# Fourteen products of zeros instead of seven, and another order of the selected branch's gathers, in a hybrid attention and state-space step

## The chip, the cores and the metric

The kernel runs on one core of one Trainium2 chip. The metric is the device time of one execution in microseconds (us), as the median of several runs. The core's engines are TensorE (PE: matrix products and transposes), VectorE (DVE), ScalarE (ACT), GpSimd (POOL) and SyncE (SP, which here only issues transfers). Each engine works through its own list of instructions in order and waits on semaphores for the others.

## The reference

One inference step of one layer for a prompt of 512 tokens and for 8 samples of 8 new tokens each, which share the weights. Cut to what matters:

```python
q, kc, vc, ksl, vsl, kwn, vwn, gn, za, u, zs, gm = split_in(h @ w_in)      # 1024 -> all parts at once
# attention of a sample: three branches, each with its own softmax
o_c = softmax(q @ compressed keys) @ compressed values      # compress(): chunks of the paged cache through a small MLP
o_s = softmax(q @ keys of the N_SEL best blocks) @ values   # "selected": rows of the second paged cache
o_w = softmax(q @ last 512 rows) @ values                   # "window"
a   = (g0 * o_c + g1 * o_s + g2 * o_w) * silu(z_att)
s   = GLU(GELU(S5(u))) * silu(z_ssm)                        # S5: complex diagonal state-space scan
x   = LayerNorm(ALPHA * x + W_o(sig(g_att) * (a @ P_att) + sig(g_ssm) * (s @ P_ssm)))
```

Everything is float32. The outputs are both groups' rows, the new key and value rows, the window's state and the S5 state.

## The kernel before, in words

All 576 rows (512 of the prompt, 64 of the samples) are held transposed. `load_x` loads five tiles `xp` of 128 rows, turns each with 8 transposes through the PSUM tile `p_tr` and splits the result into a high part `xTh` (ACT, line 108) and a low part `xTl` (DVE, line 121), because a product of float32 values is made of three products of such parts (`mm3`, `natural`). A weight tile goes the same way: `w_raw` loads `wraw` by a DMA of SP's queue (line 318; there are two such buffers), ACT makes `whi` of it, DVE `wlo`. `natural` (line 353) then makes 24 products for each row tile: four of `whi` with `xTh`, four of `whi` with `xTl`, four of `wlo` with `xTh`, and these twelve again for the second half of the inner dimension. The samples' rows take one unsplit product each (line 345, with `xTs`), straight from `wraw`.

At the very start, ahead of the first transposes, PE makes seven products of a tile `zero` of zeros (line 291) into a PSUM tile that nothing reads.

After that come, overlapping: the weights of `u` in two pieces and of the keys and values in three (`inproj_u`, `inproj_kv`; I call the last three A, B and C; the low part of B is made by POOL, and small copies `kvn`, line 390, are made by DVE in A), the S5 parameters and scan (loads at lines 490 to 509, a long chain of small operations on DVE), the rest of the in-projection, the prompt's attention (scores at lines 966 and 967), the compression of the cached pages (gathers `gc`, products at lines 129 to 131 with `evh`, `evl`), and for each pair `w` = 0 to 3 of samples `attend(w)`.

`attend(w)` handles two samples, b = 0 and 1. Its selected branch has two tiles per sample and step t, h = 0 and h = 1: `attend_gather` gathers them with four indirect DMAs of POOL's queue (line 1070) into tiles `g8`, of which five exist in all. `branch` goes through four groups; groups 0 and 1 use both samples' h = 0 tiles, groups 2 and 3 both samples' h = 1 tiles, first for the transposes of the keys (line 135) and scores (line 1192), then for the values (line 1201). A gather of step t = 1 waits until a tile of t = 0 has been read for the last time.

No order is written out by hand: the program is handed to a scheduler that sets the order of every engine's instructions from its own estimates of their durations. An edit at the start therefore moves instructions in the whole program.

Of the kernel before, what the change touches and what calls it, by code (L numbers as in the profile page):

```python
# [9 lines left out]
F = mybir.dt.float32  # L10
# [75 lines left out]
def rr(ap, pat, **kw):  # L86
    return ap.rearrange(pat, **kw)


class Hybrid:  # L90
# [41 lines left out]

    def tr(self, out, in_):
        k = in_.shape[0]
        self.nc.tensor.transpose(out, in_, self.ident[:k, :k])  # L135

    def psum(self, tag, shape, name=None):
        return self.ps.tile(shape, F, name=name or ("p_" + tag), tag=tag, bufs=self.psbufs[tag])
# [142 lines left out]
    def load_x(self):  # L281
        nc, A, pa = self.nc, self.A, self.pa
        self.xTh = pa.tile([128, 8, TOK], FR, name="xTh")
        self.xTl = pa.tile([128, 8, TOK], FR, name="xTl")
        self.xTs = pa.tile([128, 8, 64], F, name="xTs")

        z = self.p0.tile([128, 128], F, name="zero")
        nc.vector.memset(z[:], 0.0)
        p = self.psum("ca", [128, 128])
        for i in range(7):  # L290
            nc.tensor.matmul(p[:], z[:], z[:], start=True, stop=True)
        for i in range(5):
            m = 128 if i < 4 else 64
            src = rr(A["x_prompt"], "o (i p) c -> (o i) p c", p=128)[i] if i < 4 else rr(A["x_sample"], "b t c -> (b t) c")
            x = self.p0.tile([128, DM], F, name="xp", tag="xp", bufs=5)
            if i:
                nc.sync.dma_start(x[:m], src)
            else:
                for c in (slice(0, 512), slice(512, 1024)):
                    nc.sync.dma_start(x[:, c], src[:, c])  # L300
                self.wu = self.w_raw([(OFF_U, 256)], 2)
            for h in range(2):
                p = self.psum("tr", [128, 4, 128])
                for k in range(4):
                    self.tr(p[:, k, :m], x[:m, (4 * h + k) * 128:(4 * h + k + 1) * 128])
                v = slice(4 * h, 4 * h + 4), slice(i * 128, i * 128 + m)
                self.split(self.xTh[(slice(None),) + v], self.xTl[(slice(None),) + v], p[:, :, :m])
                if i == 4:
                    nc.vector.tensor_copy(self.xTs[:, 4 * h:4 * h + 4], p[:, :, :m])

# [955 lines left out]
    def attend_gather(self, w):  # L1266

        nc, A, pb = self.nc, self.A, self.pb
        wn = pb.tile([128, 2, 4, 256], F, name="wn", tag="g8", bufs=5)
        nc.gpsimd.dma_start(rr(wn[:], "q b k c -> q b (k c)"),  # L1270
                            rr(A["state_win_kv"], "b (q k) v g d -> q b (k v g d)", k=4)[:, 2 * w:2 * w + 2])
        yield wn
        for t in range(2):
            gs = []
            for b in range(2):
                for h in range(2):
                    gs.append(pb.tile([128, 8, 2, 2, 64], F, name="g8", tag="g8", bufs=5))
                    self.gather(gs[-1][:], "cache_kv_slc", self.idx2[:, h, t, 2 * w + b:2 * w + b + 1])
            yield gs[:2], gs[2:]

    def attend(self, w, store, gat):
        nc, A, pb = self.nc, self.A, self.pb
# [337 lines left out]
```

## Time and profile before

| what | value |
|---|---|
| median of 3 runs | 929.78 us (928.15 to 930.36) |
| the profiled execution | 930.57 us |
| its span, first to last instruction | 928.8 us |
| PE busy | 866.0 us, 93 % of the span |
| DVE, ACT, POOL busy | 626.4, 428.3, 224.7 us |
| mean granted TensorE clock | 0.967 of full speed |

The profiled execution's time is 1.8 us more than its span, for what lies around the instructions. PE is idle for 62.8 us of the span.

### The profile page before, as it was taken

To read this page: it belongs to the slowest core of one execution; us is meant where nothing else is said; L and a number is where in the kernel's file an instruction comes from. 1 tells how busy PE (TensorE), PEld (TensorE's weight loads), DVE (VectorE), ACT (ScalarE), POOL (GpSimd) and SP (SyncE) were. 2 spreads that over 40 slices of the span, in tenths; PEclk is the share of its full clock that TensorE was granted. 3 is DMA by queue.
4 is the path that set the end of the run, shared out by engine and by line. 5 is a ranking of instruction groups with operands and counts; after the bars stand their busy time and mean duration, and the time that the engine had idled before them with its cause. 6 is when DMAs were issued, how large, how long until landed. Compare 5 with 4: busy or idle time off the path is not lost.

```text
span 928.8 us, 18351 instructions
## 1 busy us (share of the span) xinstructions
PE 866.0 (93%) x7262; PEld 759.6 (82%) x7262; DVE 626.4 (67%) x1494; ACT 428.3 (46%) x872; POOL 224.7 (24%) x255
## 2 busy tenths in 40 slices
PE   8979999999999997999989898999999989998896
PEld 8979999899999976767777777777878778878785
DVE  3479855654444679998778777878884455347874
ACT  4214652432543546465545453555455666445410
POOL 0328285000301034211132302232321011106500
PEclk9999999999999996999999998999999989999999
DMA  8672543465962361413298627454743276756331
GB/s 267 140 202 78 163 97 103 161 207 150 297 211 72 107 207 58 147 61 98 80 323 242 232 101 273 136 177 187 272 136 123 74 260 207 257 136 197 113 102 46
DMA packets 109989, 151.02 MB, mean 163 GB/s; under 512 B 29464, under 2 KB 85128, under 8 KB 105552
## 3 DMA queue, kind: packets, MB, share of 16 engines
q1 hardware_dynamic: 84304, 69.74, 25.5%
q0 software_dynamic: 16544, 75.44, 23.2%
q10 hardware_dynamic: 9056, 4.67, 1.8%
q8 instruction: 57, 0.93, 0.4%
q14 instruction: 28, 0.23, 0.1%
HBM read 134.02 MB, written 19.93 MB: 166 GB/s over the span
## 4 chain that ended last, share of the span: by engine, by line
PE 53%; DVE 22%; DMA 11%; issue 4%; POOL 4%; ACT 4%; SPq 2%; DVEq 0%; ACTq 0%; POOLq 0%
DVE xt L872 10%; PE p_mm L130 8%; PE p_mm L129 8%; PE p_mm L131 8%; PE p_tr L135 6%; DMA g<-in_cache_kv_slc,idx 4%; PE p_S L1192 3%; DVE evl L121 3%; PE p_ca L129 2%; PE p_ca L130 2%; PE p_ca L131 2%; DMA wraw<-in_w_in 2%; DMA bt<-vD 2%; PE p_acc L1201 2%; PE p_mm L353 1%
## 5 line engine op out<-in xcount | busy, mean ns | idle before, releaser
L130 PE MATMUL p_mm<-evl,w1h 128*128 128x256 f32 (+1 forms) x512 | 156.2, 305 | 10.4 <-DVE evl L121 8.3
L129 PE MATMUL p_mm<-evh,w1h 128*128 128x256 f32 (+1 forms) x512 | 153.0, 299 | 2.1 <-ACT evh L108 2.1
L131 PE MATMUL p_mm<-evh,w1l 128*128 128x256 f32 (+1 forms) x512 | 150.7, 294 | 0.0
L872 DVE STREAM_TRANSPOSE xt<-gc 128x256 f32<-128x256 f32 x256 | 145.4, 636 | 1.5 <-DMA gc<-in_cache_kv_cmp,idx 1.0
L121 DVE TENSOR_TENSOR evl<-xt,evh 128x512 fp32r<-128x512 f32 x128 | 87.2, 687 | 55.6 <-ACT evh L108 55.2
L1070 POOL DMA_INDIRECT gc<-in_cache_kv_cmp,idx x64 | 64.2, 1004 | 246.8 <-DVE xt L872 188.4
L130 PEld LDWEIGHTS p_mm<-evl,w1h 128*128 128x128 f32 x512 | 101.5, 198 | 20.2 <-DVE evl L121 15.3
L108 ACT ACTIVATE evh<-xt 128x512 fp32r<-128x512 f32 x128 | 79.8, 628 | 80.2 <-PE p_mm L131 76.3
L129 PEld LDWEIGHTS p_mm<-evh,w1h 128*128 128x128 f32 x512 | 101.8, 199 | 8.5 <-ACT evh L108 5.4
L131 PEld LDWEIGHTS p_mm<-evh,w1l 128*128 128x128 f32 x512 | 101.7, 199 | 0.2
L129 PE MATMUL p_mm<-xTh,whi 128*128 128x288 f32 x272 | 80.8, 297 | 1.7 <-DVE zst L475 1.7
L130 PE MATMUL p_mm<-xTl,whi 128*128 128x288 f32 x272 | 81.1, 298 | 0.0
L131 PE MATMUL p_mm<-xTh,wlo 128*128 128x288 f32 x272 | 81.1, 298 | 0.0
L108 ACT ACTIVATE kt<-p_tr 128x512 f32<-128x512 f32 x72 | 41.4, 596 | 52.9 <-PE p_tr L135 52.7
L108 ACT ACTIVATE pt<-p_tr 128x512 f32<-128x512 f32 x76 | 43.0, 591 | 34.5 <-PE p_tr L135 34.5
L1070 POOL DMA_INDIRECT g<-in_cache_kv_slc,idx x32 | 30.9, 964 | 108.0 <-PE p_acc L1201 98.1
L121 DVE TENSOR_TENSOR wlo<-wraw,whi 128x2048 fp32r<-128x2048 f32 (+2 forms) x23 | 43.5, 1901 | 14.7 <-ACT whi L108 14.5
L129 PEld LDWEIGHTS p_mm<-xTh,whi 128*128 128x128 f32 x272 | 51.3, 189 | 2.0 <-DVE zst L475 2.0
L991 DVE CUSTOM_DVE_ANT_0 P<-p_S,bt 128x128 f32<-128x128 f32 (+3 forms) x64 | 30.1, 486 | 33.4 <-PE p_S L967 23.5
L130 PEld LDWEIGHTS p_mm<-xTl,whi 128*128 128x128 f32 x272 | 51.3, 189 | 0.2 <-issue 0.2
L131 PEld LDWEIGHTS p_mm<-xTh,wlo 128*128 128x128 f32 x272 | 51.4, 189 | 0.0
L108 ACT ACTIVATE whi<-wraw 128x2048 fp32r<-128x2048 f32 (+2 forms) x24 | 37.1, 1561 | 29.0 <-DMA wraw<-in_w_in 9.5
(526 smaller groups left out, 2168.0 us busy)
## 6 DMA issues: line engine op xcount, KB each, us to landing
wraw<-in_w_in SPq DMA_DIRECT2D x11, 1024.0 KB
wraw<-in_w_in SPq DMA_DIRECT2D x10, 512.0 KB
gD<-zst SPq DMA_DIRECT2D x16, 288.0 KB
tg<-gD SPq DMA_DIRECT2D x16, 288.0 KB
wn<-in_state_win_kv POOLq DMA_DIRECT2D x4, 1024.0 KB, 9.4
wor<-in_w_o SPq DMA_DIRECT2D x8, 512.0 KB
out<-in_state_win_kv SPq DMA_DIRECT2D x8, 504.0 KB
wraw<-in_w_in SPq DMA_DIRECT2D x3, 1056.0 KB
```

The costliest lines, as they stand in the source:

```text
L108: return self.nc.scalar.activation(out, in_, func, **kw)
L121: eng.tensor_tensor(lo, src, hi.bitcast(F), op=OP.subtract)
L129: mm(out, lhi, rhi, start=start, stop=False, **kw)
L130: mm(out, lhi, rlo, start=False, stop=False, **kw)
L131: mm(out, llo, rhi, start=False, stop=stop, **kw)
L135: self.nc.tensor.transpose(out, in_, self.ident[:k, :k])
L353: self.nc.tensor.matmul(p[:m, :n], a[:, k], w[:, k, :n], start=j == 0, stop=j == 23)
L872: self.nc.vector.transpose(out=out, in_=bass.AP(tensor=in_.tensor, offset=in_.offset, ap=[in_.ap[0], [1, 8], [st, 4], [8, 8]]))
L991: V.tensor_tensor_reduce(out=P4[:, r, :n], in0=p[:, :n], in1=back, scale=1.0, scalar=NEG, op0=OP.add, op1=OP.max, accum_out=mx[:, r:r + 1])
L1070: self.nc.gpsimd.indirect_dma_start(out=rr(out, "c s v g d -> c (s v g d)"), out_offset=None, in_=src, in_offset=bass.IndirectOffsetOnAxis ...
L1192: mm = self.nc.tensor.matmul(out[r], self.qb[:, w, r], keys[b], start=True, stop=True)
L1201: self.nc.tensor.matmul(acc[r], PT[:, r], vals(b)[:, g * 64:(g + 1) * 64], start=start, stop=stop, skip_group_check=True)
```

## The change

`tr` now returns its instruction. The seven products of zeros become ten, and four more are made behind the last transpose of the first row tile, held there by a dependency. `attend_gather` issues the gathers of a step in the order (b0,h0), (b1,h0), (b0,h1), (b1,h1); before it was (b0,h0), (b0,h1), (b1,h0), (b1,h1).

```diff
     def tr(self, out, in_):
         k = in_.shape[0]
-        self.nc.tensor.transpose(out, in_, self.ident[:k, :k])
+        return self.nc.tensor.transpose(out, in_, self.ident[:k, :k])
...
-        p = self.psum("ca", [128, 128])
-        for i in range(7):
-            nc.tensor.matmul(p[:], z[:], z[:], start=True, stop=True)
+        pz = self.psum("ca", [128, 128])
+
+        def warm(n, *behind):
+            for _ in range(n):
+                mm = nc.tensor.matmul(pz[:], z[:], z[:], start=True, stop=True)
+                self.after(mm, *behind)
+        warm(10)
...
-                    self.tr(p[:, k, :m], x[:m, (4 * h + k) * 128:(4 * h + k + 1) * 128])
+                    tr = self.tr(p[:, k, :m], x[:m, (4 * h + k) * 128:(4 * h + k + 1) * 128])
...
+                if i == 0 and h:
+                    warm(4, tr)
...
-            gs = []
-            for b in range(2):
-                for h in range(2):
-                    gs.append(pb.tile([128, 8, 2, 2, 64], F, name="g8", tag="g8", bufs=5))
-                    self.gather(gs[-1][:], "cache_kv_slc", self.idx2[:, h, t, 2 * w + b:2 * w + b + 1])
-            yield gs[:2], gs[2:]
+
+            gs = [[], []]
+            for h in range(2):
+                for b in range(2):
+                    gs[b].append(pb.tile([128, 8, 2, 2, 64], F, name="g8", tag="g8", bufs=5))
+                    self.gather(gs[b][-1][:], "cache_kv_slc", self.idx2[:, h, t, 2 * w + b:2 * w + b + 1])
+            yield gs
```

Lines behind `load_x` are six higher in the changed kernel (353 is 359, 318 is 324, 1070 is 1076).

The start of PE's list, before:

```order
L291 MATMUL p_ca<-zero 128x128 x7
L135 MATMUL p_tr<-cst,xp 128x128 x8
L353 MATMUL p_mm<-whi,xTh 128x256 x4
L353 MATMUL p_mm<-whi,xTl 128x256 x4
L353 MATMUL p_mm<-wlo,xTh 128x256 x4
L353 MATMUL p_mm<-whi,xTh 128x256 x4
L135 MATMUL p_tr<-cst,xp 128x128 x8
L353 MATMUL p_mm<-whi,xTl 128x256 x4
L353 MATMUL p_mm<-wlo,xTh 128x256 x4
L353 MATMUL p_mm<-whi,xTh 128x256 x4
L135 MATMUL p_tr<-cst,xp 128x128 x4
```

The same place in the changed kernel:

```order
L293 MATMUL p_ca<-zero 128x128 x10
L135 MATMUL p_tr<-cst,xp 128x128 x8
L293 MATMUL p_ca<-zero 128x128 x4
L359 MATMUL p_mm<-whi,xTh 128x256 x4
L135 MATMUL p_tr<-cst,xp 128x128 x4
L359 MATMUL p_mm<-whi,xTl 128x256 x4
L359 MATMUL p_mm<-wlo,xTh 128x256 x4
L359 MATMUL p_mm<-whi,xTh 128x256 x4
L135 MATMUL p_tr<-cst,xp 128x128 x4
L359 MATMUL p_mm<-whi,xTl 128x256 x4
L359 MATMUL p_mm<-whi,xTh 128x256 x4
L359 MATMUL p_mm<-wlo,xTh 128x256 x4
```

The second row tile's transposes have split in two and moved ahead of most of the first products, and four products of `whi` stand before the second `wlo`. On DVE the second `wlo` of this weight tile now stands behind two `xTl` instead of one.

SP's list where the third and fourth weight tiles are loaded (A and B of the keys and values), before; `a`, `dt`, `cn`, `b`, `dd` and `sn` are S5 parameters:

```order
L318 DMA wraw<-in_w_in 128x8x264
L490 DMA a_523<-in_ssm_a_re 32x64 x2
L490 DMA a_523<-in_ssm_a_im 32x64 x2
L493 DMA dt<-in_ssm_log_dt 128x32
...
L509 DMA sn<-in_state_ssm_im 128x128
L318 DMA wraw<-in_w_in 128x8x264
L664 DMA uc<-uD 32x1024 x8
L318 DMA wraw<-in_w_in 128x8x264
L664 DMA uc<-uD 8x1024 x4
```

The same place in the changed kernel:

```order
L324 DMA wraw<-in_w_in 128x8x264 x2
L496 DMA a_530<-in_ssm_a_re 32x64 x2
L496 DMA a_530<-in_ssm_a_im 32x64 x2
L499 DMA dt<-in_ssm_log_dt 128x32
...
L515 DMA sn<-in_state_ssm_im 128x128
L670 DMA uc<-uD 32x1024 x4
L324 DMA wraw<-in_w_in 128x8x264
L670 DMA uc<-uD 32x1024 x4
```

Tile B's load has moved ahead of all S5 loads, and C's load is now in front of the last four of the eight loads of `uc` (the rows of `u`, read back from memory).

POOL's list where step t = 1 of the first pair is gathered, before (`g8_5419` is b0,h0; `g8_5421` is b0,h1; `g8_5423` is b1,h0; `g8_5425` is b1,h1; `gc` are gathers of the compression):

```order
L1070 DMA g8_5419<-in_cache_kv_slc,idx2_496 128x2048
L1070 DMA gc_6769<-in_cache_kv_cmp,idx4_503 128x1024 x2
L1070 DMA gc_6772<-in_cache_kv_cmp,idx4_503 128x1024 x2
L1070 DMA g8_5421<-in_cache_kv_slc,idx2_496 128x2048
L1070 DMA g8_5423<-in_cache_kv_slc,idx2_496 128x2048
L1070 DMA g8_5425<-in_cache_kv_slc,idx2_496 128x2048
L1270 DMA wn_6289<-in_state_win_kv 128x2x1024
L1070 DMA gc_6775<-in_cache_kv_cmp,idx4_503 128x1024 x2
L1070 DMA gc_6778<-in_cache_kv_cmp,idx4_503 128x1024 x2
```

The same place in the changed kernel (`g8_5426` is b0,h0; `g8_5428` is b1,h0; `g8_5430` is b0,h1; `g8_5432` is b1,h1):

```order
L1076 DMA g8_5426<-in_cache_kv_slc,idx2_503 128x2048
L1076 DMA gc_6776<-in_cache_kv_cmp,idx4_510 128x1024 x2
L1076 DMA gc_6779<-in_cache_kv_cmp,idx4_510 128x1024 x2
L1076 DMA g8_5428<-in_cache_kv_slc,idx2_503 128x2048
L1076 DMA g8_5430<-in_cache_kv_slc,idx2_503 128x2048
L1076 DMA gc_6782<-in_cache_kv_cmp,idx4_510 128x1024 x2
L1076 DMA gc_6785<-in_cache_kv_cmp,idx4_510 128x1024 x2
L1076 DMA g8_5432<-in_cache_kv_slc,idx2_503 128x2048
L1276 DMA wn_6296<-in_state_win_kv 128x2x1024
```

The tile (b1,h0) has moved from third to second of its four, and (b1,h1) from directly behind the third to behind four more gathers of the compression. Elsewhere the order changes throughout: on PE, the first row of prompt scores (line 966 before, 972 after) moves from row 1044 to row 1242 of its list and the last from row 2046 to row 2147, while the first product of the compression moves from row 1682 to row 1650. The transposes of the S5 parameters `a` and `cn` (line 135) move from rows 63, 64 and 66 to rows 83, 91 and 95, of which most rows hold four products.

## Rows read from the trace of the kernel before

**Rows 1.** The page, busy time of TensorE.

```profile
PE 866.0 (93%) x7262; PEld 759.6 (82%) x7262; DVE 626.4 (67%) x1494; ACT 428.3 (46%) x872; POOL 224.7 (24%) x255
```

**Rows 2.** Waits of PE, whole span: total us, times, longest.

```profile
...
PE p_S L966 <- DVE amx L991: 7.8, 8, 2.8
PE p_tr L135 <- DMA g<-in_cache_kv_slc,idx: 4.9, 4, 2.3
PE p_mm L353 <- DVE kvn L390: 3.7, 1, 3.7
```

**Rows 3.** Order of time on PE, 0 to 16 us: start, duration, what.

```profile
1.06 3.36 PE L291 MATMUL p_ca<-zero 128*128 128x128 f32 x14 [1.06 <-DVE zero L288]
5.19 1.94 PE L135 MATMUL p_tr<-cst,xp 128*128 128x128 f32 x8 [0.77 <-DMA xp<-in_x_prompt]
8.84 1.22 PE L353 MATMUL p_mm<-whi,xTh 128*128 128x256 f32 x4 [1.71 <-ACT whi L108]
...
11.56 1.05 PE L353 MATMUL p_mm<-whi,xTh 128*128 128x256 f32 x4
12.42 1.77 PE L135 MATMUL p_tr<-cst,xp 128*128 128x128 f32 x8
...
14.97 0.64 PE L353 MATMUL p_mm<-whi,xTh 128*128 128x256 f32 x4
15.45 0.60 PE L135 MATMUL p_tr<-cst,xp 128*128 128x128 f32 x4
```

**Rows 4.** Order of time on ACT, 5 to 11 us.

```profile
7.73 1.06 ACT L108 ACTIVATE whi<-wraw 128x1024 fp32r<-128x1024 f32 x1 [0.82 <-DMA wraw<-in_w_in]
```

**Rows 5.** Order of time on DVE, 5 to 13 us.

```profile
9.96 0.68 DVE L121 TENSOR_TENSOR xTl<-p_tr,xTh 128x512 fp32r<-128x512 f32 x1
10.56 1.22 DVE L121 TENSOR_TENSOR wlo<-wraw,whi 128x1024 fp32r<-128x1024 f32 x1
```

**Rows 6.** Order of time on SP's queue, 30 to 66 us.

```profile
33.50 0.37 SPq L318 DMA_DIRECT2D wraw<-in_w_in  x1
...
36.50 0.42 SPq L493 DMA_DIRECT2D dt<-in_ssm_log_dt  x1
...
51.40 0.38 SPq L318 DMA_DIRECT2D wraw<-in_w_in  x1
51.97 11.69 SPq L664 DMA_DIRECT2D uc<-uD  x8
```

**Rows 7.** Order of time on PE, 38 to 73 us.

```profile
42.08 1.97 PE L345 MATMUL p_mm<-wraw,xTs 128*64 128x128 f32 x32
...
60.27 0.77 PE L353 MATMUL p_acc<-whi,xTh 128*128 128x264 f32 x4 [1.40 <-ACT whi L108]
...
65.23 1.25 PE L353 MATMUL p_mm<-whi,xTh 128*128 128x264 f32 x4 [3.73 <-DVE kvn L390]
```

**Rows 8.** Order of time on DVE and ACT, 33 to 69 us.

```profile
41.42 0.18 DVE L529 TENSOR_SCALAR w<-dt 128x32 f32<-128x32 f32 x1 [7.53 <-DMA dt<-in_ssm_log_dt]
...
58.25 1.96 ACT L108 ACTIVATE whi<-wraw 128x2112 fp32r<-128x2112 f32 x1 [6.71 <-DMA wraw<-in_w_in]
...
61.17 3.83 DVE L573 TENSOR_TENSOR w<-w,w 128x32 f32<-128x32 f32 x1
```

**Rows 9.** Busy us by stretch, PE, PEld, DVE, ACT, POOL; then granted clock.

```profile
65.10:72.00 6.90, 6.64 (x28) 6.33 (x29) 6.90 (x41) 0.09 (x1) 0.95 (x1) 0.51 0.60 190
...
350.00:400.00 50.00, 42.46 (x249) 35.96 (x249) 47.97 (x107) 27.38 (x60) 15.54 (x12) 0.81 0.29 92
```

**Rows 10.** Order of time on POOL, 515 to 545 us.

```profile
521.37 1.09 POOL L1070 DMA_INDIRECT g<-in_cache_kv_slc,idx  x1 [9.29 <-PE p_acc L1201]
522.76 0.94 POOL L1070 DMA_INDIRECT g<-in_cache_kv_slc,idx  x1 [0.30 <-issue]
...
534.22 0.94 POOL L1070 DMA_INDIRECT gc<-in_cache_kv_cmp,idx  x1 [0.30 <-issue]
```

**Rows 11.** Order of time on PE, 525 to 536 us.

```profile
531.50 1.06 PE L135 MATMUL p_tr<-cst,g 128*128 128x128 f32 x8 [2.27 <-DMA g<-in_cache_kv_slc,idx]
```

## The prediction

> **What bounds the kernel now.** The page's busy times come first: TensorE works 866.0 of 928.8 us [rows 1], so the kernel can get shorter only where PE waits (62.8 us of idle time in all) or where PE runs at its lower clock. The view of PE's waits says what it waits for: the largest that this change could touch are the gathers of the selected branch (4.9 us in 4 waits, the longest 2.3), the copy `kvn` on DVE (3.7 us, once) and the prompt's maxima on DVE (7.8 us in 8 waits) [rows 2]. Then I read four stretches in the order of time: the first 16 us [rows 3 to 5], the loads of the key and value weights around 30 to 72 us [rows 6 to 8], the stretch where prompt attention and compression overlap [rows 9], and the gathers of the first pair of samples [rows 10, 11]. All terms are set against the profiled execution, 930.57 us; it lies 0.8 us above the median of the runs shown, 929.78, so the two may be read as one number.
>
> **Term 1, the start.** Seven zero products are 14 records that take 3.36 us, 0.48 us for each product, with PE at its lower clock level [rows 3]. Four products of `whi` with `xTh` (256 columns) come 0.86 us apart at 11.56 to 12.42 and 0.48 us apart at 14.97 to 15.45 [rows 3]: that factor of about two is the change from 1.2 to 2.4 GHz, which fell inside the transposes at 12.42. So from 8.84, when the first `whi` is ready (7.73 + 1.06 = 8.79, [rows 4]), until about 13.4 PE did real work at half speed.
>
> What the added products cost: ten instead of seven last 3 x 0.48 = 1.44 us longer, so the first transposes start at about 1.06 + 4.80 = 5.86 instead of 5.19 and end at 7.80. Until 8.84 PE waited 1.71 us for `whi` anyway [rows 3], so 0.67 us of delay costs nothing there. The four new products then end at 7.80 + 1.92 = 9.7 at the lower level, 0.9 us late, or at 7.80 + 0.96 = 8.8, just in time, at the higher one.
>
> What they may bring: with the higher level from 8.84 on, 16 products (four rows of 0.86 us) and eight transposes (1.77 us) could take half as long. They cannot take all of it, since the second `wlo` now stands behind one more `xTl`: before it ended at 10.56 + 1.22 = 11.78, now about 0.7 to 0.9 us later, near 12.6 [rows 5]. PE had made the products listed up to 15.45 by then; after, those that do not need this `wlo` are done by 12.6, and the four that do end at 13.1. That is up to 15.45 - 13.1 = 2.35 us. I take **-2.0**; bounds -2.4 and +0.9.
>
> A rule speaks against this. The Trainium skill, page TensorE: Matmul & The Clock Gate, section Part 4: PE-mode transpose, says that transposes do not count as activity for the clock in the way products do. By it, the eight transposes between the ten and the four zero products (1.94 us) are a pause, the clock need not be up at 8.84, and this term would be +0.9. The trace can't decide: before, products and transposes together since 1.06 left the clock low until 13.4, but there were waits of 0.77 and 1.71 us among them.
>
> **Term 2, the key and value weights.** SP's queue issued tile A at 33.50, then the S5 parameters (17.5 us of issuing), then tile B at 51.40 [rows 6]. B's values came so late that ACT waited 6.71 us for them until 58.25 [rows 8], 6.85 us after the issue, and PE waited 1.40 us for `whi`; then 3.73 us for the copies `kvn` [rows 7], which stood on DVE behind one small S5 operation that took 3.83 us [rows 8]. After this pause PE ran at a granted clock of 0.51 from 65.10 to 72.00 [rows 9], which is 6.64 busy us of work that takes 3.3 at the full level. In all 1.40 + 3.73 + 3.3 = 8.4 us were lost here.
>
> After the change B's load stands directly behind A's. Both buffers are then in use, so SP stops there until the products of the samples' rows have read the buffer; those ended at 42.08 + 1.97 = 44.05 [rows 7], and would end at about 42 with the 2 us of term 1. Queued behind it are all S5 loads, the eight `uc` and tile C: SP is held from 33.9 to 42, and they all move by about 8 us. `dt`, on which the S5 chain on DVE started at 41.42 [rows 8], would arrive at 49.5. In return B lands at 42 + 6.85 = 49, well before PE is at it (60.27 less the 2 us of term 1: 58), and A's `kvn` copies are not behind the late S5 chain any more. So the 8.4 us can go. What is late next is C: 42 + 17.5 + 4 x 1.46 for four `uc` (11.69 / 8, [rows 6]) = 65.3 for its issue, 72.2 for its landing, 74.2 with `whi` (1.96, [rows 8]). B's 96 products at 0.12 us and its samples' products (1.97) end at 58 + 13.5 = 72, so a wait of about 2 us stands there, unless S5's transposes fill it. The best case is -8.4 + 2.2 = -6.2. Against it stands the S5 chain, up to 8 us later. PE's list puts the transposes of `a` and `cn` later as well, by 20 to 29 rows, most of four products of 0.12 us: some 10 to 14 us of PE work. So this should mostly be covered; if it isn't, PE waits up to 8 us. Nearer to the good end, because the cover is counted: **-3**; bounds -6.2 and +8.
>
> **Term 3, prompt attention and compression.** The scheduler moved most of the program: prompt attention starts 198 rows later in PE's list, compression 32 rows earlier. From 350 to 400 us DVE was busy for 47.97 of 50 us, PE for 42.46 at a granted clock of 0.81 [rows 9], and PE's 7.8 us of waits for the prompt's maxima lie around there [rows 2]. This stretch is as long as DVE's work makes it, and DVE's work is the same. Whether less or more of it comes together I can't tell. **0**; bounds -5 and +5, about two thirds of PE's 7.5 idle us there, either way.
>
> **Term 4, the gathers.** For step t = 1 a gather must wait for a free `g8`. The last three came at 521.37, 522.76 and right behind [rows 10], and PE waited 2.27 us until 531.50 for the second of them [rows 11], which is (b1,h0): 8.74 us from issue to use. In the new order (b1,h0) takes the place at 521.37, 1.39 us earlier. At two waits of about 2 us that makes 2.8, and a little at two small ones; but those products of the compression that stand between are a few less now, which takes back about 0.3 us each time. The seven added zero products have no share in this. (b1,h1) is now behind four `gc` gathers that wait for DVE; the last of these was issued at 534.22 [rows 10], so (b1,h1) is issued near 535.5 and used near 544, some 12.5 us after 531.5, and about that much of PE's work stands between. It breaks even. **-2**; bounds -4.9 (all waits gone, [rows 2]) and +2.
>
> **Sum.** -2 - 3 + 0 - 2 = -7: 930.57 - 7 = 923.6 us.
>
> **The rivals.**
> - *The held queue makes S5 late* (slower). SP's hold of 8 us reaches PE if the S5 transposes and what follows from them stand less than 8 us of PE work further back than they did. Then term 2 is up to +8 instead of -3: 930.57 - 2 + 8 - 2 = 934.6. For it: DVE had no time to spare behind 60 us, so the late chain isn't made up. Against it: PE's list has these rows later by more than 8 us. Chance 0.16.
> - *Nothing is gained* (same). The clock is still low at 8.84 (+0.9), the wait for B only moves to C and to S5 (0), and the gathers save half a wait each (-1): 930.5. For it: each gain here is a wait with another close behind. The rule of the Trainium skill named in term 1 (page TensorE: Matmul & The Clock Gate, Part 4) speaks for its first part. Chance 0.20.
> - *The overlap of prompt attention and compression gets worse*: prompt attention, which needs DVE, runs further into the compression. Decides if PE's waits for the maxima pass 13 us instead of 7.8: -7 + 5 = 928.6 alone, 933 if the start or the queue brings nothing as well. Chance 0.12, of which 0.05 is over 0.3 % slower.
> - *It gets better by as much*: 918.6. Chance 0.10.
> - *The forecast*, 923.6 and some us around it: 0.42.
>
> 0.3 % (2.8 us) is about what a measurement of this kernel can tell from no change. Faster by more than that: forecast, better overlap, and part of the third, 0.57. Within: 0.22. Slower: 0.21. The range must take in the first rival (934.6, with something on top where term 3 adds) and the better overlap (918.6, and 914 with term 2 at its best): 914 to 936.
>
> **What would show it.** Right, if the four products of 256 columns behind 8.84 us stand 0.48 us apart and no longer 0.86; if PE's wait for `kvn` and the clock of 0.51 behind it are gone and B's `whi` is ready before PE needs it; if `uc` and `dt` come about 8 us later with no new wait of PE for S5 before 160 us; if the wait for the gather of (b1,h0) is 1 us or less in each pair. Wrong, if PE waits long for C or for S5's tiles, if the granted clock drops behind such a wait, if the waits for the maxima between 350 and 450 us grow, or if (b1,h1) becomes the gather that PE waits for.

## The result and the profile after

The change makes the kernel slower. Its median of 4 runs is 965.71 us (959.74 to 966.57), against 929.88 us for the kernel before (4 runs): ratio 1.0375, 95 % interval 1.0331 to 1.0419. The forecast of 923.6 us and its whole range, 914 to 936, are missed on the slow side. The profiled execution took 966.57 us with a span of 964.8 us, 36.0 us longer than before, at a mean granted clock of 0.952 (0.967 before).

The page after, to set beside [rows 1]:

```profile
PE 878.0 (91%) x7276; PEld 771.5 (80%) x7276; DVE 630.8 (65%) x1494; ACT 430.0 (45%) x872; POOL 229.0 (24%) x255
```

PE has 14 records more (7 products of zeros) and is busy 12.0 us longer. About 2.3 us of that are the added products ([rows 3] and their rows under term 1 below: 4.63 + 1.06 - 3.36); the rest goes with the lower clock, since busy time multiplied by the granted clock is 837 us before and 836 after. PE's idle time grew from 62.8 to 86.8 us. The other engines are busy for about as long as before. PE's waits after, to set beside [rows 2] (total us, times, longest):

```profile
PE p_mm L130 <- DVE evl L121: 22.9, 19, 2.8
PE p_mm L129 <- ACT oh L108: 5.6, 1, 5.6
PE p_acc L1207 <- issue: 5.4, 10, 1.1
PE p_acc L1207 <- ACT pt L108: 5.0, 4, 1.7
...
PE p_S L972 <- DVE amx L997: 3.3, 6, 1.5
...
PE p_tr L135 <- DMA g<-in_cache_kv_slc,idx: 1.4, 1, 1.4
```

All three waits that the prediction named shrank: `kvn` is gone, the gathers went from 4.9 to 1.4 us, the maxima from 7.8 to 3.3. In their place stands `evl`, the low part of the compression's tiles, which DVE makes: 22.9 us in 19 waits. Before:

```profile
PE p_mm L130 <- DVE evl L121: 8.3, 15, 1.8
```

This wait is not a measure of the loss: `fill6`, a kernel below that takes as long as the one before, waits 16.2 us for `evl`, and `zero20`, which loses 15 us, waits 10.3.

Where the time went is read by stretches. I cut the span at 100, 300 and 450 us and then at the last value product of the selected branch of each pair of samples (w = 0 to 3). First before, then after; the columns are those of [rows 9] (us, busy us of PE, PEld, DVE, ACT, POOL; granted clock; then the busy share of the DMA engines and GB/s).

```profile
0.00:100.00 100.00, 91.21 (x750) 86.69 (x752) 65.70 (x177) 34.70 (x59) 38.70 (x49) 0.97 0.61 170
100.00:300.00 200.00, 195.68 (x1556) 190.72 (x1552) 109.97 (x229) 80.29 (x179) 43.24 (x73) 1.00 0.54 164
300.00:450.00 150.00, 137.17 (x878) 112.57 (x876) 125.22 (x313) 85.64 (x197) 33.29 (x32) 0.92 0.36 113
450.00:568.00 118.00, 110.09 (x1032) 88.75 (x1031) 87.41 (x225) 59.28 (x115) 31.72 (x32) 0.96 0.62 209
568.00:660.00 92.00, 85.62 (x893) 71.23 (x891) 72.86 (x184) 47.44 (x94) 24.80 (x25) 0.98 0.54 190
660.00:744.00 84.00, 79.93 (x858) 66.77 (x856) 53.90 (x147) 45.38 (x91) 12.66 (x13) 0.98 0.39 137
744.00:837.00 93.00, 87.07 (x889) 74.21 (x877) 45.59 (x111) 48.98 (x88) 12.61 (x12) 0.96 0.68 216
```

```profile
0.00:100.00 100.00, 91.11 (x789) 86.71 (x789) 61.25 (x172) 30.84 (x54) 31.95 (x35) 1.00 0.66 185
100.00:300.00 200.00, 197.23 (x1538) 193.84 (x1539) 108.59 (x196) 81.71 (x165) 55.33 (x89) 0.98 0.54 165
300.00:450.00 150.00, 129.78 (x857) 106.74 (x857) 129.00 (x337) 84.13 (x205) 32.44 (x31) 0.93 0.31 101
450.00:594.00 144.00, 128.59 (x1087) 103.15 (x1088) 97.68 (x258) 65.61 (x129) 30.39 (x32) 0.91 0.51 170
594.00:699.00 105.00, 92.07 (x928) 77.69 (x916) 77.74 (x194) 49.21 (x97) 29.12 (x29) 0.93 0.52 187
699.00:787.00 88.00, 79.59 (x838) 66.65 (x834) 48.48 (x132) 49.17 (x93) 8.95 (x9) 0.94 0.37 134
787.00:873.00 86.00, 80.42 (x842) 67.97 (x831) 42.23 (x94) 42.83 (x80) 13.13 (x12) 0.96 0.65 212
```

Call a stretch's loss its length less PE's busy time times the granted clock: what PE lost idle or at the lower level. For 450 to 568 us before it is 118 - 110.09 x 0.96 = 12.3 us. (The clock has two digits, so each loss is good to about half a per cent of its stretch. In the first 16 us before, the view gives a granted clock of 1.00, while the products' spacing in [rows 3] shows half speed until about 13.4 us; some 2 us of loss are missing there.)

| stretch | loss before | loss after | difference |
|---|---|---|---|
| 0 to 100 us | 11.5 | 8.9 | -2.6 |
| 100 to 300 us | 4.3 | 6.7 | +2.4 |
| 300 to 450 us | 23.8 | 29.3 | +5.5 |
| 450 us to the end of w0, w1, w2, w3 | 12.3 + 8.1 + 5.7 + 9.4 = 35.5 | 27.0 + 19.4 + 13.2 + 8.8 = 68.4 | +32.9 |

The differences come to +38.2 us; the span grew by 36.0, the stretch behind w3 is as long as before (91.8 us), and the rest lies within the rounding. The first 100 us, where the change was made, gained. Nearly the whole 36 us were lost between 450 and 787 us, in the sample attention and what of the compression runs beside it, which have one line of the change in them (the gathers' order) and none of the zeros.

### The profile page after: what moved, and what is told of

Same layout as the page of the kernel before. It is cut to its first block, busy times and chain, and to the rows that moved or that the text cites. A ratio compares the mean times of both kernels' runs of the same rounds, so it can differ in the third digit from the quotient of the medians.

```text
span 964.8 us, 18375 instructions
## 1 busy us (share of the span) xinstructions
PE 878.0 (91%) x7276; PEld 771.5 (80%) x7276; DVE 630.8 (65%) x1494; ACT 430.0 (45%) x872; POOL 229.0 (24%) x255
## 4 chain that ended last, share of the span: by engine, by line
PE 59%; DVE 18%; DMA 6%; ACT 4%; POOL 4%; issue 4%; SPq 3%; ACTq 0%; DVEq 0%; POOLq 0%
PE p_mm L130 10%; PE p_mm L131 10%; PE p_mm L129 9%; DVE xt L878 8%; PE p_tr L135 6%; PE p_S L1198 3%; PE p_acc L1207 3%; DVE evl L121 3%; PE p_ca L130 3%; PE p_ca L129 3%; PE p_ca L131 2%; ACT P L108 2%; DMA relx<-in_rel_bias 1%; POOL X L788 1%; DVE P L997 1%
## 5 line engine op out<-in xcount | busy, mean ns | idle before, releaser
L130 PE MATMUL p_mm<-evl,w1h 128*128 128x256 f32 (+1 forms) x512 | 158.7, 310 | 25.8 <-DVE evl L121 22.9
L129 PE MATMUL p_mm<-evh,w1h 128*128 128x256 f32 (+1 forms) x512 | 155.7, 304 | 1.3 <-ACT evh L108 1.3
L131 PE MATMUL p_mm<-evh,w1l 128*128 128x256 f32 (+1 forms) x512 | 153.2, 299 | 0.0
L130 PEld LDWEIGHTS p_mm<-evl,w1h 128*128 128x128 f32 x512 | 103.9, 203 | 37.9 <-DVE evl L121 33.8
L129 PEld LDWEIGHTS p_mm<-evh,w1h 128*128 128x128 f32 x512 | 104.3, 204 | 4.9 <-ACT evh L108 3.3
L131 PEld LDWEIGHTS p_mm<-evh,w1l 128*128 128x128 f32 x512 | 104.4, 204 | 1.0 <-issue 0.8
L108 ACT ACTIVATE pt<-p_tr 128x512 f32<-128x512 f32 x76 | 42.6, 591 | 40.7 <-PE p_tr L135 35.5
L135 PE MATMUL p_tr<-cst,P 128*128 128x128 f32 x304 | 50.0, 299 | 7.7 <-ACT P L108 3.9
L135 PEld LDWEIGHTS p_tr<-cst,P 128*128 128x128 f32 x304 | 37.7, 151 | 21.6 <-issue 10.1
```

The costliest lines, as they stand in the source:

```text
L108: return self.nc.scalar.activation(out, in_, func, **kw)
L129: mm(out, lhi, rhi, start=start, stop=False, **kw)
L130: mm(out, lhi, rlo, start=False, stop=False, **kw)
L131: mm(out, llo, rhi, start=False, stop=stop, **kw)
L135: return self.nc.tensor.transpose(out, in_, self.ident[:k, :k])
```

## The experiments

**Which part costs it: `warm_only`, `gather_only`, `after_4only`, `zero10`.** The kernel before took 926.44 us on this chip.

```diff
 warm_only   (from after):   gathers of a step in the old order again
 gather_only (from before):  gathers of a step in the new order
 after_4only (from after):   -warm(10)               +warm(7)
 zero10      (from before):  -for i in range(7):     +for i in range(10):
```

> The products of zeros alone (ten, and four behind the first row tile's transposes), with the gathers in their old order. The scheduler's order of this kernel differs from that of before nearly as much as that of the whole change. Theory A (the loss comes from the order that the scheduler makes once the start is longer): about as slow as the whole change, 950 to 966 us, with the +12 us near 340 us and the waits for evl (22.9 us in the whole change, 8.3 before) back again. Theory B (the loss of 25 to 30 us that gathers between 440 and 760 us is the new order of the gathers): about 936 us, with the lag of some 6 us that the whole change had by 440 us and no more behind it.

> The new order of the gathers alone, seven products of zeros. The order of all engines is that of before up to the first selected-branch gathers. Theory A: 924 to 930 us, since the waits of PE for the gathers (4.9 us before, 1.4 in the whole change) get shorter and nothing else moves. Theory B: 950 to 960 us, the lag growing from about 500 us on.

> The whole change with seven products ahead instead of ten, the four behind the transposes kept. The scheduler keeps the order of before for this one up to the gathers, and that of the run with the gathers alone behind. Theory A: within 3 us of the run with the gathers alone. Theory C (the products of zeros themselves cost the time, by the clock or by PE's list): as slow as the whole change, or a good part of it.

> The kernel before with ten products of zeros instead of seven, nothing behind the transposes and the old gathers. Its order is that of the run with all products of zeros but for five rows of PE's list. Theory A: as the run with all the products of zeros, 950 to 966 us. If the four products behind the transposes are what matters (theory C): near 930 us.

| kernel | us | ratio, 95 % interval |
|---|---|---|
| `warm_only` | 953.44 | 1.0291 (1.0257 to 1.0324) |
| `gather_only` | 931.96 | 1.0063 (1.0041 to 1.0085) |
| `after_4only` | 930.38 | 1.0052 (1.0032 to 1.0072) |
| `zero10` | 956.13 | 1.0328 (1.0286 to 1.0371) |

Three products of zeros, 1.44 us by [rows 3], cost 30 us. The gathers' new order costs 0.6 %; the four products behind the transposes add nothing that shows to that (`after_4only` against `gather_only`).

**Is it the products, or the order the scheduler makes around them: `zero7_4`, `zero20`, `g_w012_7_4`, `zero10_b`.** (Before: 927.0 us.) `zero10_b` holds tile B's load back, in the program's order, until the last S5 load has been issued.

```diff
 zero7_4    (from before):  the change's warm(), with warm(7) and warm(4, tr); old gathers
 zero20     (from before):  -for i in range(7):  +for i in range(20):
 g_w012_7_4 (from zero7_4): new gather order for w < 3 only
 zero10_b   (from zero10; self.snd is the last S5 load):
-            raw = self.w_raw([(OFF_KV + 264 * j, 264)])
+            with (self.tc.issue_after(self.snd.ins) if j == 1 else ExitStack()):
+                raw = self.w_raw([(OFF_KV + 264 * j, 264)])
```

> Seven products of zeros as before, the four behind the first row tile's transposes added, old order of the gathers. The scheduler's order is that of before but for four rows of PE's list, so this measures term 1 alone. My theory: the first products of whi run at 2.4 GHz (0.48 us apart instead of 0.86) and the kernel takes 1.5 to 2.5 us less than before. Rival: the start's gain is taken back where PE next waits for a load (no change, within 0.7 us). If the four products themselves did harm: slower by 1 us or more.

> Twenty products of zeros ahead and nothing else changed. With these the scheduler falls into a third order, in which prompt attention and compression stand to each other as before (93 of the compression's products ahead of the last prompt scores, as before; 125 in the order of ten products). Theory A (the order costs the time): 925 to 936 us, though there are twice as many products as in the run with ten. Theory C (the products cost): slower than the run with ten, 956 us or more.

> The new order of the gathers for the first three pairs of samples only, seven products of zeros ahead and the four behind the transposes. In the run with the new order for all pairs and the same products, PE was ahead of before by 5 to 7 us from 580 to 720 us and lost it in the tail. If the tail's loss comes from the last pair's gathers, this keeps the lead: 920 to 924 us. If the lead is lost because the output stage's weights come no earlier (the wait for oh grows by what PE gained), it is 928 to 931 us as with all pairs.

> Ten products of zeros, and the load of tile B of the key and value weights held behind the S5 loads, as before. The scheduler makes a fourth order of it: prompt attention starts 100 rows later in PE's list than before instead of 195, and 85 of the compression's products stand ahead of the last prompt scores (93 before, 125 with ten products and B's load ahead). If what costs is that compression has run ahead of prompt attention, which the early load of B brings about: 928 to 938 us, the +12 us near 340 us mostly gone. If the load has no part in it: about 956 us.

| kernel | us | ratio, 95 % interval |
|---|---|---|
| `zero7_4` | 926.63 | 0.9992 (0.9967 to 1.0017) |
| `zero20` | 941.73 | 1.0156 (1.0108 to 1.0203) |
| `g_w012_7_4` | 929.73 | 1.0018 (0.9996 to 1.0039) |
| `zero10_b` | 948.9 | 1.0230 (1.0193 to 1.0267) |

Eleven products in all cost nothing (`zero7_4`), ten cost 30 us, twenty cost half of that. A price that falls when the work doubles is not the work's. `zero7_4` keeps the order of before but for its four rows; `zero10` and `zero20` each get an order of their own. With B's load back behind the S5 loads a quarter of the loss returns (21.9 us are left of 29.7), although S5 is then about on time: its first product on PE (line 682) starts at 92.47 us, 91.29 before. This kernel pays some 4 us of its own in the first 100 us, where PE waits 7.2 us for B's `whi`.

**Real lateness or order: `zero10_s5pool`, `after_s5pool`, `zero10_s5act`, `before_s5late`.** (Before: 930.23 us.) In the first three, SP's queue no longer carries the S5 loads (six source lines). `before_s5late` has the seven products of before, and its first S5 load must wait for a product that has read the samples' rows.

```diff
 zero10_s5pool (from zero10), after_s5pool (from after), in all six lines of S5 loads:
-            nc.sync.dma_start(a4[:, j, :], A[nm])
+            nc.gpsimd.dma_start(a4[:, j, :], A[nm])
 zero10_s5act (from zero10): the same with nc.scalar
 before_s5late (from before; self.last_xts is the last such product):
-            nc.sync.dma_start(a4[:, j, :], A[nm])
+            d = nc.sync.dma_start(a4[:, j, :], A[nm])
+            if j == 0:
+                self.after(d, self.last_xts)
```

> Ten products of zeros as in the run that took 956 us, but the loads of the S5 parameters (lines 490 to 509) go through POOL's queue instead of SP's, so that they don't stand behind tile B of the key and value weights. The scheduler's order is then nearly that of before: 433 products of the in-projection ahead of the first prompt scores (433 before, 497 with ten products and SP's queue), 93 of the compression's ahead of the last prompt scores (93; 125). Theory S5 (the loads held behind tile B make S5 late, prompt attention late behind it, and spend the in-projection that should lie beside it): 923 to 932 us. Theory C (ten products cost): about 956 us.

> The whole change with the S5 loads on POOL's queue; the scheduler's order then has the figures of before (433 and 93). Theory S5: nearly all of the change's loss goes, 925 to 934 us, the rest being the new order of the gathers, which cost 0 to 5 us by itself. If the loss has other causes too: 940 us or more.

> Ten products of zeros, the S5 loads on ACT's queue: on the chip they come early, but the scheduler keeps the long order (497 of the in-projection ahead of the first prompt scores, 125 of the compression's ahead of the last). If it is the order of the lists that costs: 948 to 960 us. If it is the real lateness of S5's data on the chip: 925 to 935 us.

> Seven products of zeros, old gathers; the first S5 load waits for the samples' products of the second u tile (ended at 44.05 us before), which is what tile B's load makes the whole queue wait for in the change. The scheduler answers with 465 products of the in-projection ahead of the first prompt scores (433 before, 497 in the change), as in the run with ten products and B's load held. Theory S5: 940 to 952 us, though no product of zeros was added. Rival (only the start's products or the gathers matter): 925 to 930 us.

| kernel | us | ratio, 95 % interval | S5 chain on DVE starts | first S5 product on PE |
|---|---|---|---|---|
| `zero10_s5pool` | 933.8 | 1.0058 (1.0031 to 1.0086) | 53.14 us | 97.20 us |
| `after_s5pool` | 936.63 | 1.0066 (1.0041 to 1.0091) | 50.79 us | 93.49 us |
| `zero10_s5act` | 966.76 | 1.0386 (1.0329 to 1.0443) | 52.45 us | 100.01 us |
| `before_s5late` | 959.94 | 1.0328 (1.0274 to 1.0381) | 41.44 us | 100.28 us |

The fourth column is the first operation of DVE that reads `dt`: 41.42 us before [rows 8], 53.87 in `zero10`. The last is the first product of `wg` with `U`, which needs nearly the whole chain: 91.29 us before, 103.86 in `zero10`.

`before_s5late` has no product added, and loses 30 us. By `dt` its S5 chain is on time, but the chain as a whole is not: the scheduler set the one held load behind nearly all other S5 loads, so it was issued at 50.24 us instead of 33.91, PE waited for it, and the first S5 product comes 9 us late. SP's queue and PE's order of time in it:

```profile
50.24 0.37 SPq L490 DMA_DIRECT2D a<-in_ssm_a_re  x1
```

```profile
51.85 0.32 PE L135 MATMUL p_S<-cst,a 32*128 32x32 f32 x2 [1.79 <-DMA a<-in_ssm_a_re]
```

So this kernel doesn't have the order without the lateness. What speaks against the lateness as the cause is `zero10_s5pool`: its chain starts as late as that of `zero10` (53.14 and 53.87 us), its first S5 product is 6 us later than before, and it loses 0.6 %. `zero10_s5act` was meant to have S5 early; it was late too, so it separates nothing. The stretches of `before_s5late`, cut in the same way:

```profile
0.00:100.00 100.00, 91.16 (x756) 86.49 (x756) 62.13 (x172) 32.43 (x55) 33.33 (x37) 0.97 0.66 185
100.00:300.00 200.00, 197.01 (x1560) 194.06 (x1561) 111.78 (x217) 84.46 (x184) 51.16 (x87) 0.99 0.51 161
300.00:450.00 150.00, 137.49 (x874) 106.08 (x873) 126.21 (x329) 84.64 (x198) 32.70 (x31) 0.95 0.33 107
450.00:577.00 127.00, 115.20 (x1083) 95.90 (x1082) 97.72 (x246) 60.66 (x118) 33.19 (x33) 0.96 0.58 197
577.00:686.00 109.00, 93.69 (x912) 78.19 (x911) 76.66 (x194) 49.48 (x97) 29.82 (x30) 0.92 0.51 184
686.00:775.00 89.00, 78.59 (x829) 65.55 (x828) 48.83 (x133) 48.88 (x92) 8.37 (x10) 0.95 0.35 125
775.00:861.00 86.00, 80.32 (x832) 67.80 (x831) 41.99 (x92) 42.47 (x80) 13.02 (x12) 0.96 0.64 210
```

Up to 450 us its losses are 11.6 + 5.0 + 19.4 = 36.0, against 11.5 + 4.3 + 23.8 = 39.6 before: the late S5 has cost nothing that is left by then. From there on they are 16.4 + 22.8 + 14.3 + 8.9 = 62.4 against 35.5. `zero10_s5pool` stays near before in the same four stretches (the last four rows):

```profile
0.00:100.00 100.00, 86.26 (x699) 81.74 (x700) 63.11 (x169) 30.01 (x50) 41.38 (x62) 0.93 0.56 160
...
450.00:572.00 122.00, 113.67 (x1063) 91.97 (x1061) 92.42 (x237) 61.91 (x120) 31.31 (x32) 0.97 0.59 201
572.00:664.00 92.00, 84.62 (x891) 69.48 (x883) 72.15 (x182) 47.34 (x94) 24.26 (x25) 1.00 0.54 194
664.00:748.00 84.00, 79.41 (x887) 65.99 (x875) 54.28 (x147) 45.27 (x91) 12.66 (x13) 1.00 0.40 139
748.00:840.00 92.00, 86.19 (x873) 73.54 (x866) 45.99 (x111) 49.12 (x89) 12.60 (x12) 0.98 0.66 217
```

That is 11.7 + 7.4 + 4.6 + 7.5 = 31.2. Its 0.6 % is itself a sum: in the first 100 us it loses 19.8 us against 11.5, where PE waits 5.7 us for `kvn`, and most of that comes back behind 300 us.

**What in the order costs it: `fill6`, `fill7`, `fill8`.** (Before: 929.68 us.) The orders differ in how many products of the in-projection stand ahead of the first prompt score in PE's list: 433 before, 497 in `zero10`. These kernels, with seven zeros, set that number by hand to 431, 461 and 493.

```diff
...
-                self.inproj_rest(0, 2)
+                self.inproj_rest(0, 7)     # 6 in fill6, 8 in fill8
+                self.last_rest = self.last_mm
...
-                self.inproj_rest(2, 12)
+                self.inproj_rest(7, 12)
...
+        if q == g == r == 0 and not self.held:
+            self.held = True
+            self.after(m0, self.last_rest)
```

> The first prompt score waits for the last product of the sixth weight tile of the rest of the in-projection, seven products of zeros, S5 loads and gathers as before. 431 products of the in-projection stand ahead of the first prompt scores (before: 433). Both theories: about the time of before, 924 to 934 us; it is the control of the two others.

> As fill6, but the first prompt score waits for the seventh tile: 461 products of the in-projection ahead of it. Theory filler (these products are what PE does while prompt attention waits for DVE, and spent ahead they are missing beside it): 6 to 15 us more than fill6, with waits of PE around 320 to 350 us. Theory other (something else in the change's order): within 4 us of fill6.

> As fill6, but the first prompt score waits for the eighth tile: 493 products of the in-projection ahead of it (497 in the whole change). Theory filler: 15 to 30 us more than fill6. Theory other: within 6 us of fill6.

| kernel | products ahead | us | ratio, 95 % interval |
|---|---|---|---|
| `fill6` | 431 | 928.49 | 0.9992 (0.9967 to 1.0018) |
| `fill7` | 461 | 943.8 | 1.0142 (1.0087 to 1.0198) |
| `fill8` | 493 | 929.45 | 1.0016 (0.9991 to 1.004) |

The theory falls: the largest number costs nothing, the middle one 14 us. `fill7` is the cleanest case of order alone: it has no added product, its loads stand as before and its S5 is on time (first product at 90.36 us, 91.29 before).

**The gathers of the compression: `zero10_hold`, `after_hold`, `before_hold2`.** (Before: 926.14 us.) One figure sorted all kernels so far: how many gathers of the compression POOL's list has ahead of each pair's window gather. Before it is 28, 8, 16 and 12, after it is 28, 12, 16 and 8. The last of the four is 12 in each kernel within 0.7 % of before and 8 in each slower one; the others vary (24, 12, 16, 12 in `fill6`; 26, 14, 16, 8 in `zero10_b` and `before_s5late`). The first two kernels here force 28, 8, 16, 12 on `zero10` and on the whole change; the third goes further the same way on before (28, 6, 16, 14).

```diff
-            self.gather(out[-1][:, t % 2], "cache_kv_cmp", self.idx4[:, t, b:b + 1])
+            with (self.tc.issue_after(self.wnd[b // 2 - 1].ins) if b in (4, 6) and t >= 4 else ExitStack()):
+                self.gather(out[-1][:, t % 2], "cache_kv_cmp", self.idx4[:, t, b:b + 1])
...
-        nc.gpsimd.dma_start(rr(wn[:], "q b k c -> q b (k c)"),
+        self.wnd[w] = nc.gpsimd.dma_start(rr(wn[:], "q b k c -> q b (k c)"),
```

In `before_hold2` the condition is `t >= 2`.

> Ten products of zeros with their slow order (956 us), but four gathers of the compression are held behind the window gather of pair 1, and four behind that of pair 2: POOL's list has 28, 8, 16, 12 of them between the pairs, as before. Everything up to the attention of the samples stays as in the run with ten. Theory supply (compression's products are what PE does while the sample attention waits, and in the slow order they run out sooner): 930 to 942 us. If the figure only goes along with the true cause: 950 us or more.

> The whole change with the same two holds. Theory supply: 935 to 948 us instead of 966, some of it left to the gathers' order in the last pair. Otherwise: 958 us or more.

> The kernel before, with six gathers held behind each of the two window gathers instead of four: 28, 6, 16, 14. If more of the compression left for the last pairs helps further: 918 to 926 us. If PE then runs dry in the first pair instead, or the compression becomes late for its own pair: 930 us or more.

| kernel | us | ratio, 95 % interval |
|---|---|---|
| `zero10_hold` | 972.06 | 1.0465 (1.0398 to 1.0531) |
| `after_hold` | 960.12 | 1.0357 (1.0298 to 1.0415) |
| `before_hold2` | 949.46 | 1.0257 (1.0194 to 1.032) |

The whole change keeps its loss with the good figure, and `zero10` loses 16 us more. The figure goes along with the loss and is not its cause. `before_hold2` is slower, but it too got a new order throughout, so it says nothing of the gathers by themselves.

No kernel beat the one before by more than its interval.

## Why the prediction was wrong

**The step that failed** is term 3 with what it left out. "The scheduler moved most of the program", it said, and then priced one stretch of it, 350 to 400 us, at "**0**; bounds -5 and +5", because "DVE's work is the same". In that stretch the loss fell from 15.6 to 11.5 us, but the poor part of the overlap had only moved ahead, to 300 to 350 us, where it rose from 2.9 to 13.9. First before, then after:

```profile
300.00:350.00 50.00, 48.05 (x331) 40.88 (x330) 33.35 (x100) 26.33 (x70) 10.26 (x12) 0.98 0.46 149
```

```profile
300.00:350.00 50.00, 41.96 (x280) 36.30 (x280) 40.41 (x109) 24.58 (x70) 15.52 (x13) 0.86 0.35 113
350.00:400.00 50.00, 41.45 (x270) 34.44 (x270) 44.70 (x117) 26.61 (x64) 9.38 (x11) 0.93 0.30 96
```

Over 300 to 450 us that is +5.5, just past the bound. The rest of the moved program, above all the sample attention from 450 us on, had no price but the gathers of term 4, which is nothing for a reorder of everything. It cost +32.9 us. The same work in another order is not the same time: from 450 us to the end of w3, DVE's busy time is about the same before and after (259.8 and 266.1 us), but PE's idle time grew from 24.3 to 42.3 us and its clock fell. Two of the rivals named a wait that could grow; none let it cost more than 8 us. (The lower end of the range has a slip that changes nothing: the better overlap with term 2 at its best is 918.6 - 3.2 = 915.4, not 914.)

How far this is shown: order alone costs 14 us, with nothing added and S5 on time (`fill7`). Added products alone cost nothing (`zero7_4`), and S5 late without the bad order costs 0.6 % (`zero10_s5pool`, by 6 us; in the changed kernel it is 10). So the first rival, S5 late on the chip, gave the right sign, but for a reason that accounts for little. `before_hold2`, with S5 on time (90.96 us) and no product added, loses 23 us, of which its holds may have a share. That order alone makes up the whole 30 to 36 us is the best reading, and no clean run shows it: every kernel that lost 27 us or more had S5 late as well. The order hangs on where the S5 loads are: with them on POOL's queue the whole change costs 0.66 % instead of 3.75 %. That their place behind tile B in SP's list is what sets it off isn't shown, since holding B back returned only a quarter and `zero10_s5act`, with them on ACT's queue, keeps the loss. Which move within the order costs the time stays open: two candidates were tried, and both fell. That `evl` is waited for goes along with the loss only roughly: from 450 us to the end of w3 it is 7.6 us before, 12.1 after and 12.5 in `fill6`, which loses nothing.

**Term 1** (-2.0): half right. PE's order of time after:

```profile
5.49 1.09 PE L135 MATMUL p_tr<-cst,xp 128*128 128x128 f32 x8
6.41 1.06 PE L293 MATMUL p_ca<-zero 128*128 128x128 f32 x8
9.90 0.73 PE L359 MATMUL p_mm<-whi,xTh 128*128 128x256 f32 x4 [2.43 <-ACT xTh L108]
...
14.93 0.60 PE L135 MATMUL p_tr<-cst,xp 128*128 128x128 f32 x4
```

The clock came up earlier, as wanted: the eight transposes took 1.09 us, 1.94 before, and the first real products start at the higher level (0.73 us for four, 1.22 before) in spite of a wait of 2.43 us. But they start 1.06 us later than the 8.84 of [rows 3], because PE waits for `xTh`, and the transposes of 15.45 stand at 14.93: 0.5 us, not 2. In `zero10`, without the four products behind the transposes, the wait is 3.13 us and the clock is low behind it (granted 0.50 from 9.5 to 16 us):

```profile
9.93 1.22 PE L353 MATMUL p_mm<-whi,xTh 128*128 128x256 f32 x4 [3.13 <-ACT xTh L108]
```

By the Trainium skill, page TensorE: Matmul & The Clock Gate, section Part 4: PE-mode transpose, transposes do not count as activity for the clock in the way products do; `zero10` and after agree with it, but the wait differs as well, so no run here shows which of the two it was. By the samples' products the lead is gone (42.17 us, 42.08 before [rows 7]), and `zero7_4`, which has the four products in the order of before, gains nothing that can be measured.

**Term 2** (-3): the mechanism went as worked out, with two of its sizes off. SP's queue after, to set beside [rows 6]:

```profile
33.60 10.95 SPq L324 DMA_DIRECT2D wraw<-in_w_in  x2
...
48.06 0.95 SPq L499 DMA_DIRECT2D dt<-in_ssm_log_dt  x1
...
64.56 0.40 SPq L324 DMA_DIRECT2D wraw<-in_w_in  x1
```

SP was held from 33.60 to 44.55 (forecast 42, because the 2 us of term 1 never reached the samples' products). C was issued at 64.56 (forecast 65.3), which is partly luck: the four `uc` ahead of it took 1.8 us and not 5.8, which hid the longer hold. `dt` is read at 52.58 us instead of 41.42, 11 us late (forecast 8), the wait for `kvn` and the clock of 0.51 behind it are gone (granted 1.00 from 57 to 73 us), and the new wait for C is there, 2.15 us where about 2 was forecast, but for `wlo` and not for `whi`:

```profile
77.91 0.76 PE L359 MATMUL p_mm<-wlo,xTh 128*128 128x264 f32 x4 [2.15 <-DVE wlo L121]
...
101.10 1.96 PE L687 MATMUL p_S<-U,wg 128*128 128x72 f32 x8 [2.00 <-ACT wg L108]
```

Terms 1 and 2 together are the -2.6 us of the first 100 us, where -5 stood. Then comes the second row's wait, of 2.00 us, for an S5 tile; the forecast had no such wait before 160 us. ACT, which makes that tile, had itself waited 3.60 us for a weight tile before it. The granted clock is 0.66 from 100 to 110 us (1.00 before), so what was gained at `kvn` is in part lost again there.

**Term 4** (-2): right about the waits, wrong about the sum. `gather_only`, which has nothing else of the change, cut them from 4.9 to 0.6 us, and its pair w2 ends near 736 instead of 744 us. But its last pair takes longer:

```profile
...
PE p_mm L129 <- ACT oh L108: 4.9, 1, 4.9
...
PE p_tr L135 <- DMA g<-in_cache_kv_slc,idx: 0.6, 2, 0.3
```

```profile
652.40:735.80 83.40, 80.34 (x871) 67.28 (x864) 53.38 (x144) 45.30 (x90) 12.02 (x13) 0.98 0.39 138
735.80:837.00 101.20, 90.66 (x894) 77.07 (x882) 48.17 (x112) 48.94 (x89) 13.01 (x12) 0.93 0.62 202
```

101.2 us instead of 93, with a loss of 101.2 - 90.66 x 0.93 = 16.9 instead of 9.4. The lead is given back there, and the median is 0.6 % up. The last pair's own gathers are not the reason: `g_w012_7_4`, which gathers the last pair in the old order, has the same long pair,

```profile
737.40:837.20 99.80, 88.83 (x878) 75.65 (x877) 47.37 (x108) 48.40 (x88) 12.70 (x12) 0.95 0.64 202
```

with a loss of 15.4 us and the same wait for `oh`, 4.9 us against 3.4 before. It starts 7 us earlier than before and ends at the same time, so the gathers' waits were not what the end waits for; what is, stays open. The ratio of 1.0018 with the old order in the last pair, against 1.0052 with the new one (`after_4only`), is no clear difference, since the intervals overlap.

## What to carry to other kernels

Where a scheduler sets the order from its own estimates, an edit of 1.5 us can cost 30 us: when the order printed for the change differs far behind the edit, every reordered stretch needs bounds of its own, and here each of the first three pairs of samples lost 7 to 15 us more. To tell a part's own price from the price of the new order, time the part in a kernel that keeps the old order (`zero7_4`, `zero10_s5pool`), and the order in a kernel without the part (`fill7`). A kernel built for that must be read by all that hangs on the edit: in `before_s5late` `dt` is on time and `a` is not. A wait that a change removes is a gain only if the last stretch of the kernel ends earlier; look there first.

## What the runs showed of the hardware that was not expected

PE can be held up between small products with nothing in the profile that it waits for. In the changed kernel, the value products of one selected group, 64 in number, which take 1.10 us elsewhere, took over 5 us:

```profile
544.11 0.76 PE L1207 MATMUL p_acc<-g,pt 128*32 128x64 f32 x38
545.04 0.32 PE L1207 MATMUL p_acc<-g,pt 128*32 128x64 f32 x5 [0.17 <-issue]
546.47 0.30 PE L1207 MATMUL p_acc<-g,pt 128*32 128x64 f32 x3 [1.11 <-issue]
547.19 0.22 PE L1207 MATMUL p_acc<-g,pt 128*32 128x64 f32 x1 [0.42 <-issue]
...
549.32 0.65 PE L1207 MATMUL p_acc<-g,pt 128*32 128x64 f32 x12 [0.45 <-issue]
```

They start again about 0.72 us apart, or twice that. Such waits come to 5.4 us in all here, 4.8 in `before_s5late`, 5.8 in `fill7` and 7.2 in `zero10_s5act`, to 1.2 to 1.9 us in four kernels with little loss (`fill6`, `fill8` and the two with S5 on POOL's queue), and the view of PE's waits lists none before or in the others. In the changed kernel they fall in two places, 543 to 552 and 694 to 700 us, in both of which the DMA engines were busy for 0.97 of the time. The cause was not tried, and it can't be that of the whole loss, since `zero10` loses its 30 us without any.
